# A hybrid decoder step on one core: another way to sum one layer norm's variance, and plain products for one feature pair

## The chip, the cores and the metric

The kernel runs on one core of one Trainium2 chip. The metric is device time in microseconds (us): 1178.86 us, the median of three runs (1178.64 to 1180.99). TensorE is called PE in the profile (PEld is its weight load), VectorE DVE, ScalarE ACT, GpSimd POOL, and SyncE SP, which here issues all DMAs.

## What is computed

One layer of a decoder on 1024 prompt positions and 32 sample positions (8 sequences of 4), model width 1024. Cut to what matters here:

```python
mixed = concat([rms_norm(y_lru, g_lru), rms_norm(y_attn, g_attn)])   # width 1024
y_mix = mixed @ w_out + b_out
h1 = layer_norm(ALPHA * x + y_mix, ln1_g, ln1_b)                     # "first norm"
hid = silu(h1 @ w_gate) * (h1 @ w_up)                                # 2816 features
h2 = layer_norm(ALPHA * h1 + hid @ w_down, ln2_g, ln2_b)
```

`layer_norm` subtracts the mean over the 1024 features, divides by the root of the mean square plus 1e-5, scales and shifts.

## The kernel before, in words

Features lie on the 128 partitions and positions along the free dimension, so a 1024-wide row of activations is eight tiles, `y1[m, s]`. There are two chunks of positions: chunk 0 with 512 positions, chunk 1 with 544 (512 prompt, 32 sample), the latter often handled in two halves of 272, named `10` and `1272`.

Nearly every product is done in three matmuls. An operand is split into a rounded high part (a copy into the type fp32r, by ACT or DVE) and the rest as low part (a subtraction, by POOL or DVE), and `three` adds high by high, high by low and low by high. A split therefore costs one copy and one subtraction.

The order of work: input projections, attention and recurrence; the output projection of chunk 0 and then of chunk 1 (`out_stream`, banks `ps_o`); the first norm of each chunk (`layer_norm1`) followed by `right_factors`; gate and up projection by feature pairs (`gate_up`); the down projection with the second norm (`last_sums`, `norm2`). The first norm of chunk 0 falls into the output projection of chunk 1. The first norm of chunk 1 has no such cover but the first feature pair of chunk 0: `EARLY = 2` lets features 0 and 1 of chunk 0 be done alone, then come features 0 and 1 of chunk 1 alone, then all later pairs with both chunks.

A feature pair is a 256 x 1024 block of weights times the 1024-wide activations. `gate_up` does it by a seven-product scheme: both sides are cut in 2 x 2 blocks, and seven products of sums of blocks (`a11`, `s2`, `s1`, `a12`, `s3`, `s4`, `a22` on the left; `b11`, `e`, `t1`, `b21`, `t3`, `b22`, `t4` on the right), each of four steps of 128, are combined by DVE (`take`). `right_factors` makes the right blocks of one chunk: for each `k` of 0 to 3 it takes the tiles `x = y1[k]` and `y = y1[k + 4]`, forms `t1` and `e` (tile `rf..u`) and `t3` and `t4` (`rf..v`) by four additions or subtractions of half a tile, and splits `y`, `u`, `v` and half of `x`.

In the first norm, `mean_square` sums over the partitions by one matmul with a matrix of 1/1024 (`ones`) and leaves the mean in PSUM (`ps_m1`). DVE centres the eight tiles, ACT squares them, POOL or DVE adds the squares up, and `rstd` brings the sum to one value per position (matmuls with one column each, a root and a reciprocal on small tiles, four small diagonals, and a matmul that spreads the result over the partitions in PSUM, `v1_.._b`). DVE then multiplies the eight tiles by it.

Nothing is issued as written. The functions record operations; a planner (`Recorder.order`) then plays the program through with a cost per operation, a due time taken from the order of matmuls, and the number of buffers, and fixes the order on every engine. `nc.tt` may go to POOL or DVE and `nc.copy` to ACT or DVE: the first engine named is home, and the planner leaves it when it would be late there. The costs know nothing of one engine slowing another. Since one line issues everything (L417), all rows of the profile have that line, and one goes by the names of tiles. In the profile the names are shortened (`x7_b` to `x_b`, `x7_t` to `x_t`, `v1` to `v`).

Buffers that play a part: 73 slots of tag `g` for activations; `wh` and `wl`, two each, for split weights; `wr` (4) and `wq` (5) for raw weights; three PSUM banks `mm`, two `s`, two `tp`.

## Time and profile before

| | |
|---|---|
| median of the runs | 1178.86 us |
| profiled execution, its own time | 1177.26 us |
| its span, first to last instruction | 1175.5 us |
| mean granted clock of TensorE | 0.966 |
| busy: PE, PEld | 1096.3 us (93%), 1020.7 us (87%) |
| busy: DVE, ACT, POOL | 695.3 us (59%), 569.6 us (48%), 767.0 us (65%) |

The busy shares are means over stages with different limits. The granted clock is a share of 2.4 GHz; the two levels are 1.0 and 0.5, and a value between them is a mean over a stretch. DVE and POOL durations hold also the time in which an instruction stands on its engine and can't go on.

### The profile page before, as it was taken

How to read it: one execution, taken by the hardware profiler on the slowest of the kernel's cores; microseconds unless marked ns; L12 is line 12 of the kernel's file. 1: busy time of each engine (PE TensorE's matmuls, PEld its weight loads, DVE VectorE, ACT ScalarE, POOL GpSimd, SP SyncE). 2: the span in 40 equal slices, each digit the busy share in tenths (PEclk: the TensorE clock that was granted, in tenths of full speed). 3: DMA queues.
4: the chain of work that ended last, by engine and by line, in shares of the span. 5: the costliest groups of instructions: out<-in, count | busy, mean ns of one | idle time of the engine just before them, and what ended most of it. 6: DMA issues, size and time to landing. Idle time of an engine off the chain costs nothing.

```text
span 1175.5 us, 20650 instructions
## 1 busy us (share of the span) xinstructions
PE 1096.3 (93%) x7546; PEld 1020.7 (87%) x7546; DVE 695.3 (59%) x1332; ACT 569.6 (48%) x1096; POOL 767.0 (65%) x687
## 2 busy tenths in 40 slices
PE   9789998987998966899999999999999999999996
PEld 7578888875777965899999999999999888899996
DVE  6998847899877599833333324333335644376654
ACT  6578836687744346433233223323335433465553
POOL 7844464566756977898878877887889936501100
PEclk9999999999899968899999999999999999999998
DMA  8420012244133413234223323322338636566561
GB/s 290 148 73 20 27 56 76 76 142 126 64 124 110 136 55 113 91 108 160 99 87 118 127 73 110 118 100 83 119 124 302 209 117 212 159 205 207 180 200 48
DMA packets 83813, 146.59 MB, mean 125 GB/s; under 512 B 12112, under 2 KB 16368, under 8 KB 83696
## 3 DMA queue, kind: packets, MB, share of 16 engines
q1 hardware_dynamic: 83712, 145.28, 37.5%
q8 instruction: 59, 0.97, 0.4%
q14 instruction: 42, 0.34, 0.1%
HBM read 121.75 MB, written 21.80 MB: 122 GB/s over the span
## 4 chain that ended last, share of the span: by engine, by line
PE 64%; DVE 7%; issue 1%; ACT 0%; POOL 0%; DVEq 0%; ACTq 0%
PE ps_d L417 22%; PE ps_o L417 5%; PE ps_7g L417 3%; PE ps_1u L417 3%; PE ps_4g L417 3%; PE ps_6u L417 3%; PE ps_5u L417 3%; PE ps_4u L417 3%; PE ps_3u L417 3%; PE ps_3g L417 3%; PE ps_7u L417 3%; PE ps_2u L417 3%; PE ps_1g L417 3%; PE ps_6g L417 3%; PE ps_5g L417 2%; PE ps_2g L417 2%
## 5 line engine op out<-in xcount | busy, mean ns | idle before, releaser
L417 PE MATMUL ps_d<-hid_h,wd 128*128 128x272 f32 (+1 forms) x1056 | 245.2, 325 | 0.0
L417 PEld LDWEIGHTS ps_d<-hid_h,wd 128*128 128x128 f32 x1056 | 176.7, 188 | 16.0 <-issue 0.5
L417 DVE SCALAR_TENSOR_TENSOR wd<-wd_r,wmean,wd 128x512 fp32r<-128x512 f32 x132 | 116.2, 916 | 107.9 <-ACT wd L417 107.6
L417 PE MATMUL ps_d<-hid_l,wd 128*128 128x272 f32 (+1 forms) x528 | 170.3, 325 | 0.0
L417 ACT ACTIVATE wd<-wd_r,wmean 128x512 fp32r<-128x512 f32 x132 | 90.4, 719 | 93.1 <-PE ps_d L417 83.9
L417 PEld LDWEIGHTS ps_d<-hid_l,wd 128*128 128x128 f32 x528 | 99.0, 188 | 8.4 <-issue 0.5
L417 POOL TENSOR_TENSOR var<-var,q_l 128x272 f32<-128x272 f32 (+1 forms) x17 | 19.6, 1151 | 116.9 <-ACT q_l L417 83.2
L417 POOL TENSOR_TENSOR hid_l<-hr,hid_h 128x512 fp32r<-128x512 f32 (+1 forms) x44 | 63.2, 1451 | 11.9 <-ACT hid_h L417 8.8
L417 PE MATMUL ps_o<-mix_h,wo_h 128*128 128x272 f32 (+1 forms) x192 | 66.6, 350 | 1.3 <-DVE y L417 1.3
L417 PE MATMUL ps_o<-mix_l,wo_h 128*128 128x272 f32 (+1 forms) x192 | 63.6, 333 | 0.6 <-POOL mix_l L417 0.6
L417 PE MATMUL ps_o<-mix_h,wo_l 128*128 128x272 f32 (+1 forms) x192 | 63.8, 334 | 0.1
L417 POOL TENSOR_TENSOR up<-sg,up 128x512 f32<-128x512 f32 (+1 forms) x44 | 59.9, 1362 | 0.0
L417 ACT ACTIVATE p<-p,st 128x257 f32<-128x257 f32 (+3 forms) x104 | 49.5, 490 | 14.6 <-DVE st L417 14.1
L417 POOL TENSOR_TENSOR wo_l<-wo_r,wo_h 128x512 fp32r<-128x512 f32 x31 | 41.7, 1360 | 16.1 <-ACT wo_h L417 16.1
L417 PEld LDWEIGHTS ps_o<-mix_h,wo_h 128*128 128x128 f32 x192 | 37.4, 195 | 4.6 <-DVE y L417 1.5
L417 POOL TENSOR_TENSOR sum<-sum,y 128x272 f32<-128x272 f32 (+1 forms) x33 | 35.6, 1091 | 8.2 <-DVE y L417 7.9
L417 PEld LDWEIGHTS ps_o<-mix_l,wo_h 128*128 128x128 f32 x192 | 37.4, 195 | 3.6 <-POOL mix_l L417 0.8
L417 PE MATMUL ps_1g<-x_b,wg_a11p 128*128 128x256 f32 (+1 forms) x264 | 35.9, 290 | 4.9 <-DVE x_b L417 2.4
L417 PE MATMUL ps_2g<-x_b_h,wg_a12p 128*128 128x272 f32 (+1 forms) x176 | 35.0, 290 | 5.2 <-DVE up L417 5.2
L417 ACT CAST hid_h<-hr 128x512 fp32r<-128x512 f32 (+1 forms) x44 | 27.4, 631 | 25.3 <-DMA hr<-hid 24.5
L417 PEld LDWEIGHTS ps_o<-mix_h,wo_l 128*128 128x128 f32 x192 | 36.9, 192 | 3.0 <-DVE wo_l L417 0.3
L417 DVE TENSOR_TENSOR up<-up,ps_6u 128x256 f32<-128x256 f32 (+1 forms) x22 | 9.4, 428 | 50.1 <-PE ps_6u L417 46.2
(514 smaller groups left out, 3777.0 us busy)
## 6 DMA issues: line engine op xcount, KB each, us to landing
wd_r<-in_dram SPq DMA_DIRECT2D x132, 256.0 KB, 3.0
wg_a<-in_dram SPq DMA_DIRECT2D x48, 256.0 KB, 3.0
wu_a<-in_dram SPq DMA_DIRECT2D x48, 256.0 KB, 2.7
wm<-in_dram SPq DMA_DIRECT2D x44, 256.0 KB, 3.3
wo_r<-in_dram SPq DMA_DIRECT2D x32, 256.0 KB, 2.9
hid<-up SPq DMA_DIRECT2D x22, 272.0 KB, 2.1
hr<-hid SPq DMA_DIRECT2D x22, 272.0 KB, 3.1
hid<-up SPq DMA_DIRECT2D x22, 256.0 KB, 2.1
```

What stands on the lines that cost most here:

```text
L417: getattr(getattr(self.nc, op.eng), op.fn)(*[real(a) for a in op.args], **{k: real(v) for k, v in op.kw.items()})
```

## The change

Two things change. In the first norm of chunk 1 (`if s:`) the squares go straight into matmuls with the 1/1024 matrix, eight accumulated in one PSUM bank; a root over the full 128 x 272 tile on ACT, and a reciprocal on DVE, give the factor as a tile in SBUF. Chunk 0 keeps the old way. And the first feature pair of chunk 0 is done by `gate_up0`: for gate and up and each of the two features, eight plain products of 128 x 128 weights with 512 positions, whose right operands are the split rows (`rows`). So `right_factors(0)` splits whole rows of `x`, not half of them; all the other splits stay, since later pairs still use the seven products. The subtractions of the splits in `right_factors` now have DVE as home, for both chunks.

```diff
--- before.py
+++ after.py
@@ -1197,10 +1197,10 @@
 
     MIX_ORDER = (4, 5, 6, 7, 0, 1, 2, 3)
 
-    def split(dst, y, o, n):
+    def split(dst, y, o, n, first="gpsimd"):
         h, l = dst
         nc.copy(h[:, o : o + n], y)
-        nc.tt(l[:, o : o + n], y, h[:, o : o + n].bitcast(F32), op=ALU.subtract)
+        nc.tt(l[:, o : o + n], y, h[:, o : o + n].bitcast(F32), op=ALU.subtract, first=first)
 
     y1 = {}
     sums = {}
@@ -1241,22 +1241,37 @@
 
         nm = f"{s}{o}"
         mu = mean_square(sums[s, o][:, :n], n, f"ps_m1_{nm}")
-        s2 = [temp(f"v{i}_{nm}") for i in range(2)]
-        for m in range(8):
-            y = y1[m, s][:, o : o + n]
-            i = m % 2
-            nc.vector.scalar_tensor_tensor(y, y, bcen[:, m : m + 1], mu[:, :n], op0=ALU.add, op1=ALU.subtract)
-            q = s2[i] if m < 2 else temp(f"q{m}_{nm}")
-            nc.scalar.activation(q[:, :n], y, AF.Square)
-            if m >= 2:
-                nc.tt(s2[i][:, :n], s2[i][:, :n], q[:, :n], op=ALU.add)
-            if m % 3 == 2:
-                yield
-        nc.tt(s2[0][:, :n], s2[0][:, :n], s2[1][:, :n], op=ALU.add, first="vector")
-        s2 = s2[0]
-        yield
-        r = rstd(s2[:, :n], n, f"v1_{nm}", 1.0, 1e-5)
-        yield
+        if s:
+            var = acc(f"ps_v1_{nm}", pss, "s")
+            for m in range(8):
+                y = y1[m, s][:, o : o + n]
+                nc.vector.scalar_tensor_tensor(y, y, bcen[:, m : m + 1], mu[:, :n], op0=ALU.add, op1=ALU.subtract)
+                q = temp(f"q{m}_{nm}")
+                nc.scalar.activation(q[:, :n], y, AF.Square)
+                nc.tensor.matmul(var[:, :n], ones, q[:, :n], start=(m == 0), stop=(m == 7))
+                if m % 3 == 2:
+                    yield
+            yield
+            r = temp(f"r1_{nm}")
+            nc.scalar.activation(r[:, :n], var[:, :n], AF.Sqrt, bias=col("eps", 1))
+            nc.vector.reciprocal(r[:, :n], r[:, :n])
+        else:
+            s2 = [temp(f"v{i}_{nm}") for i in range(2)]
+            for m in range(8):
+                y = y1[m, s][:, o : o + n]
+                i = m % 2
+                nc.vector.scalar_tensor_tensor(y, y, bcen[:, m : m + 1], mu[:, :n], op0=ALU.add, op1=ALU.subtract)
+                q = s2[i] if m < 2 else temp(f"q{m}_{nm}")
+                nc.scalar.activation(q[:, :n], y, AF.Square)
+                if m >= 2:
+                    nc.tt(s2[i][:, :n], s2[i][:, :n], q[:, :n], op=ALU.add)
+                if m % 3 == 2:
+                    yield
+            nc.tt(s2[0][:, :n], s2[0][:, :n], s2[1][:, :n], op=ALU.add, first="vector")
+            s2 = s2[0]
+            yield
+            r = rstd(s2[:, :n], n, f"v1_{nm}", 1.0, 1e-5)
+            yield
         for m in range(8):
             y = y1[m, s][:, o : o + n]
             nc.vector.tensor_tensor(y, y, r[:, :n], op=ALU.mult)
@@ -1275,6 +1290,7 @@
     normed = [0, 0]
     seven = {}
     kept = {}
+    rows = {}
 
     def right_factors(s):
 
@@ -1291,14 +1307,21 @@
             nc.tt(t4, b21, e, op=ALU.subtract)
             for nm, r in ((("b21", "b22"), y), (("t1", "e"), u), (("t3", "t4"), v)):
                 h, l = slot(f"x7_{nm[0]}{k}{s}_h", F32R), slot(f"x7_{nm[0]}{k}{s}_l", F32R)
-                split((h, l), r[:, :n], 0, n)
+                split((h, l), r[:, :n], 0, n, "vector")
+                if nm[0] == "b21":
+                    rows[k + 4] = h, l
                 for i in range(2):
                     c = slice(i * hw, (i + 1) * hw)
                     seven[nm[i], k, s] = (h[:, c], l[:, c])
-            x7 = slot(f"x7_b11{k}{s}", F32R)
-            h, l = seven["b11", k, s] = (x7[:, :hw], x7[:, hw:n])
-            nc.copy(h, b11)
-            nc.tt(l, b11, h.bitcast(F32), op=ALU.subtract)
+            if s:
+                x7 = slot(f"x7_b11{k}{s}", F32R)
+                h, l = seven["b11", k, s] = (x7[:, :hw], x7[:, hw:n])
+                nc.copy(h, b11)
+                nc.tt(l, b11, h.bitcast(F32), op=ALU.subtract, first="vector")
+            else:
+                rows[k] = slot(f"x7_b1{k}_h", F32R), slot(f"x7_b1{k}_l", F32R)
+                split(rows[k], x[:, :n], 0, n, "vector")
+                seven["b11", k, s] = tuple(r[:, :hw] for r in rows[k])
             for m in (k, k + 4):
                 d = kept[m, s] = spill.tile([P, n], F32, tag=f"y{m}{s}", name=f"keep{m}{s}")
                 nc.sync.dma_start(d, y1[m, s][:, :n])
@@ -1407,6 +1430,35 @@
                 nc.tt(u[s][i], g[s][i], u[s][i], op=ALU.mult)
                 d = hid[f + i, s] = spill.tile([P, SC[s][1]], F32, tag=f"h{f + i}{s}", name=f"hid{f + i}{s}")
                 nc.sync.dma_start(d, u[s][i])
+
+    def gate_up0(f):
+
+        n = SC[0][1]
+        yield 0
+        while 7 not in rows or ("b11", 3, 0) not in seven:
+            tick()
+        g = {}
+        for x, w in (("g", w_g), ("u", w_u)):
+            for i in range(2):
+                ps = bank(f"ps_e{x}{f + i}")
+                for j in range(2):
+                    p, t, c = ((pw, "wr", 4), (pg2, "wq", 5))[j]
+                    r = p.tile([P, HW], F32, tag=t, name=f"we{x}{f + i}{j}_r", bufs=c)
+                    nc.sync.dma_start(r, w[f + i][:, j * HW : (j + 1) * HW])
+                    h, l = piece(f"we{x}{f + i}{j}")
+                    nc.copy(h, r)
+                    nc.tt(l, r, h.bitcast(F32), op=ALU.subtract)
+                    for k in range(4):
+                        c = slice(k * P, (k + 1) * P)
+                        yield three(ps, n, h[:, c], l[:, c], *(q[:, :n] for q in rows[4 * j + k]), j + k == 0,
+                                    j + k == 4)
+                if x == "g":
+                    g[i] = slot(f"sg{f + i}0")[:, :n]
+                    nc.scalar.activation(g[i], ps[:, :n], AF.Silu)
+                else:
+                    nc.vector.tensor_tensor(g[i], g[i], ps[:, :n], op=ALU.mult)
+                    d = hid[f + i, 0] = spill.tile([P, n], F32, tag=f"h{f + i}0", name=f"hid{f + i}0")
+                    nc.sync.dma_start(d, g[i])
 
     def row_mean(f):
 
@@ -1582,7 +1634,7 @@
     def means(f):
         return later(lambda: [row_mean(f + i) for i in range(2)])
 
-    streams += [gate_up(f, (0,)) for f in range(0, EARLY, 2)] + [later(settle)]
+    streams += [gate_up0(f) for f in range(0, EARLY, 2)] + [later(settle)]
     for f in range(0, FT, 2):
         streams += [gate_up(f, both if f >= EARLY else (1,)), means(f)]
     streams += [last_sums(*b) for b in LAST]
```

The planner gives another order. On PE, at the end of the output projection (`ps_o711` is its last bank, the first rows here), the products of chunk 0's pair follow: seven-product banks `ps_1g`, `ps_6g` before, plain banks `ps_eg0` now, with the means `ps_m1` and the sums of squares `ps_v1` of chunk 1's two halves. Before:

```order
L417 MATMUL ps_o711_4704<-mix31_l_3738,wo71_h_4585 128x272
L417 MATMUL ps_o711_4704<-mix31_h_3627,wo71_l_4599 128x272
L417 MATMUL ps_1g00_0_4743<-x7_b1100_4320,wg00_a11p_4661 128x256 x3
L417 MATMUL ps_1g00_0_4743<-x7_b1110_4386,wg00_a11p_4661 128x256 x3
L417 MATMUL ps_1g00_0_4743<-x7_b1120_4415,wg00_a11p_4661 128x256 x3
L417 MATMUL ps_1g00_0_4743<-x7_b1130_4430,wg00_a11p_4661 128x256 x3
L417 MATMUL ps_6g00_0_4769<-x7_t100_h_4405,wg00_s2p_4669 128x256
L417 MATMUL ps_6g00_0_4769<-x7_t100_l_4674,wg00_s2p_4669 128x256
L417 MATMUL ps_6g00_0_4769<-x7_t100_h_4405,wg00_s2p_4669 128x256
L417 MATMUL ps_m1_10_4775<-sum_10_4240,oi_206 128x272
L417 MATMUL ps_m1_1272_4780<-sum_1272_4266,oi_206 128x272
```

And now:

```order
L417 MATMUL ps_o711_4718<-mix31_h_3627,wo71_l_4628 128x272
L417 MATMUL ps_eg0_4749<-x7_b10_h_4316,weg00_4680 128x512
L417 MATMUL ps_eg0_4749<-x7_b10_l_4336,weg00_4680 128x512
L417 MATMUL ps_eg0_4749<-x7_b10_h_4316,weg00_4680 128x512
L417 MATMUL ps_m1_10_4760<-sum_10_4236,oi_206 128x272
L417 MATMUL ps_eg0_4749<-x7_b11_h_4339,weg00_4680 128x512
L417 MATMUL ps_eg0_4749<-x7_b11_l_4357,weg00_4680 128x512
L417 MATMUL ps_eg0_4749<-x7_b11_h_4339,weg00_4680 128x512
L417 MATMUL ps_eg0_4749<-x7_b12_h_4367,weg00_4680 128x512
L417 MATMUL ps_eg0_4749<-x7_b12_l_4383,weg00_4680 128x512
L417 MATMUL ps_eg0_4749<-x7_b12_h_4367,weg00_4680 128x512
L417 MATMUL ps_m1_1272_4779<-sum_1272_4262,oi_206 128x272
```

The place of the means is nearly the same; all plain products of the pair (96 with 512 columns) and the 16 of the variance stand before the first product of chunk 1.

On DVE, around the last two evacuations of the output projection (`y1_71<-..ps_o710`, `ps_o711`) and the first centring of chunk 1 (`y1_01<-..ps_m1_10`). Before:

```order
L417 SCALAR_TENSOR_TENSOR y1_71_4062<-y1_71_4062,ps_o710_4658 128x272
L417 TENSOR_TENSOR x7_t310_l_4720<-rf10v_4671,x7_t310_h_4688 128x512
L417 TENSOR_TENSOR sum_10_4240<-sum_10_4240,y1_71_4062 128x272
L417 TENSOR_TENSOR x7_t320_l_4732<-rf20v_4609,x7_t320_h_4716 128x512
L417 SCALAR_TENSOR_TENSOR y1_71_4062<-y1_71_4062,ps_o711_4704 128x272
L417 TENSOR_TENSOR x7_t110_l_4757<-rf10u_4423,x7_t110_h_4531 128x512
L417 TENSOR_TENSOR rf00v_4767<-y1_40_3179,rf00u_4324 128x256
L417 TENSOR_TENSOR x7_b2110_l_4773<-y1_50_3195,x7_b2110_h_4461 128x512
L417 TENSOR_TENSOR x7_t130_l_4784<-rf30u_4508,x7_t130_h_4764 128x512
L417 TENSOR_TENSOR rf30v_4602<-y1_70_3218,rf30u_4508 128x256
L417 TENSOR_TENSOR wg00_s4_4794<-wg00_s2_4637,wg00_a12_4561 128x512
L417 SCALAR_TENSOR_TENSOR y1_01_3295<-y1_01_3295,ng2_314,ps_m1_10_4775 128x272
```

And now:

```order
L417 TENSOR_TENSOR x7_t300_l_4634<-rf00v_4598,x7_t300_h_4624 128x512
L417 SCALAR_TENSOR_TENSOR y1_61_4060<-y1_61_4060,ps_o610_4607 128x272
L417 SCALAR_TENSOR_TENSOR y1_61_4060<-y1_61_4060,ps_o611_4647 128x272
L417 TENSOR_TENSOR x7_t310_l_4705<-rf10v_4618,x7_t310_h_4697 128x512
L417 SCALAR_TENSOR_TENSOR y1_71_4065<-y1_71_4065,ps_o710_4678 128x272
L417 SCALAR_TENSOR_TENSOR y1_71_4065<-y1_71_4065,ps_o711_4718 128x272
L417 SCALAR_TENSOR_TENSOR y1_01_3295<-y1_01_3295,ng2_314,ps_m1_10_4760 128x272
L417 SCALAR_TENSOR_TENSOR y1_11_3329<-y1_11_3329,ng2_314,ps_m1_10_4760 128x272
L417 SCALAR_TENSOR_TENSOR y1_21_3390<-y1_21_3390,ng2_314,ps_m1_10_4760 128x272
L417 SCALAR_TENSOR_TENSOR y1_31_3427<-y1_31_3427,ng2_314,ps_m1_10_4760 128x272
L417 SCALAR_TENSOR_TENSOR y1_41_3684<-y1_41_3684,ng2_314,ps_m1_10_4760 128x272
L417 SCALAR_TENSOR_TENSOR y1_01_3295<-y1_01_3295,ng2_314,ps_m1_1272_4779 128x272
```

The splits of chunk 0's right factors (`x7_..`) and a sum for the weights (`wg00_s4`), which stood between the two, are gone from there; fourteen of chunk 0's splits stand earlier, among the evacuations from `y1_21` on.

On PE, where the last split of chunk 1's right factors (`x7_t331_l`) is used, in product 7 of gate; products 3 and 4 follow. Before:

```order
L417 MATMUL ps_7g01_1_5351<-x7_t331_h_5319,wg01_s3p_5289 128x272
L417 MATMUL ps_7g01_1_5351<-x7_t331_l_5348,wg01_s3p_5289 128x272
L417 MATMUL ps_7g01_1_5351<-x7_t331_h_5319,wg01_s3p_5289 128x272
L417 MATMUL ps_3g01_1_5371<-x7_b2101_h_5232,wg01_s4p_5327 128x272
L417 MATMUL ps_3g01_1_5371<-x7_b2101_l_5271,wg01_s4p_5327 128x272
```

And now:

```order
L417 MATMUL ps_3g01_1_5211<-x7_b2121_h_5139,wg01_s4p_5171 128x272
L417 MATMUL ps_3g01_1_5211<-x7_b2121_l_5165,wg01_s4p_5171 128x272
L417 MATMUL ps_7g01_1_5167<-x7_t331_l_5222,wg01_s3p_5136 128x272
L417 MATMUL ps_7g01_1_5167<-x7_t331_h_5194,wg01_s3p_5136 128x272
L417 MATMUL ps_3g01_1_5211<-x7_b2121_h_5139,wg01_s4p_5171 128x272
L417 MATMUL ps_3g01_1_5211<-x7_b2131_h_5145,wg01_s4p_5171 128x272
L417 MATMUL ps_3g01_1_5211<-x7_b2131_l_5185,wg01_s4p_5171 128x272
L417 MATMUL ps_3g01_1_5211<-x7_b2131_h_5145,wg01_s4p_5171 128x272
L417 MATMUL ps_4g01_1_5248<-x7_t301_h_5153,wg01_a22p_5188 128x272
```

Behind that split there stood 26 matmuls up to the end of product 4 (`ps_4g01`, twelve of 272 columns), and now 18: part of product 3 has moved ahead.

## Rows read from the trace of the kernel before

**Rows 1.** Windows: PE, PEld, DVE, ACT, POOL busy (count), granted clock, DMA share, GB/s.
```profile
372.00:397.00 25.00, 25.00 (x183) 23.97 (x184) 8.11 (x16) 13.90 (x25) 19.93 (x23) 0.93 0.49 167
397.00:411.00 14.00, 13.48 (x109) 13.27 (x108) 13.66 (x14) 3.43 (x7) 13.95 (x12) 1.00 0.39 112
411.00:447.00 36.00, 25.30 (x131) 22.43 (x129) 35.63 (x61) 18.44 (x43) 27.30 (x24) 0.67 0.14 45
447.00:478.00 31.00, 18.40 (x102) 16.44 (x103) 31.00 (x47) 19.28 (x35) 23.01 (x20) 0.78 0.33 115
433.45:436.87 3.42, 3.42 (x20) 3.42 (x19) 3.42 (x5) 1.10 (x3) 2.79 (x3) 0.50 0.24 77
500.00:520.00 20.00, 20.00 (x166) 20.00 (x166) 5.84 (x14) 7.53 (x14) 19.73 (x16) 1.00 0.29 100
```

**Rows 2.** Chain of work that ended last, pieces in order of time.
```profile
474.98 1.80 DVE x_t_l L417
...
480.71 1.66 PE ps_4g L417 x12
...
899.98 2.93 PE ps_4u L417 x24
```

**Rows 3.** Timeline of DVE: start us, duration us, instruction, count.
```profile
412.77 0.42 DVE L417 SCALAR_TENSOR_TENSOR y<-y,ps_o 128x272 f32<-128x272 f32 x1
...
419.45 1.71 DVE L417 SCALAR_TENSOR_TENSOR y<-y,ng,ps_m 128x272 f32<-128x272 f32 x4
...
440.25 2.87 DVE L417 TENSOR_TENSOR y<-y,v_b 128x272 f32<-128x272 f32 x8 [0.37 <-PE v_b L417]
...
452.97 0.42 DVE L417 TENSOR_TENSOR y<-y,v_b 128x272 f32<-128x272 f32 x1
...
477.04 1.47 DVE L417 TENSOR_TENSOR x_t_l<-rf31v,x_t_h 128x544 fp32r<-128x544 f32 x1
```

**Rows 4.** Timeline of POOL, around the end of the output projection.
```profile
397.44 2.81 POOL L417 TENSOR_TENSOR wo_l<-wo_r,wo_h 128x512 fp32r<-128x512 f32 x2
...
413.28 1.14 POOL L417 TENSOR_TENSOR sum<-sum,y 128x272 f32<-128x272 f32 x1 [1.93 <-DVE y L417]
```

**Rows 5.** Groups by form, DVE, 419.4 to 478.5 us: busy us, mean ns.
```profile
L417 DVE SCALAR_TENSOR_TENSOR y<-y,ng,ps_m 128x272 f32<-128x272 f32 x16 | 6.8, 486 | 0.0
...
L417 DVE TENSOR_TENSOR y<-y,v_b 128x272 f32<-128x272 f32 x16 | 5.9, 427 | 0.4 <-PE v_b L417 0.4
...
L417 DVE TENSOR_TENSOR x_b<-y,x_b 128x272 fp32r<-128x272 f32 x3 | 3.0, 999 | 0.0
...
L417 DVE TENSOR_TENSOR wg_s3p<-wg_s,wg_s3p 128x512 fp32r<-128x512 f32 x2 | 2.5, 1228 | 0.0
...
L417 DVE TENSOR_TENSOR x_b_l<-y,x_b_h 128x544 fp32r<-128x544 f32 x3 | 2.1, 712 | 0.0
...
L417 DVE TENSOR_TENSOR x_t_l<-rf11v,x_t_h 128x544 fp32r<-128x544 f32 x1 | 1.8, 1804 | 0.0
...
L417 DVE TENSOR_TENSOR rf11v<-y,rf11u 128x272 f32<-128x272 f32 x1 | 1.6, 1575 | 0.0
...
L417 DVE TENSOR_TENSOR rf21v<-y,y 128x272 f32<-128x272 f32 x1 | 0.4, 429 | 0.0
...
L417 DVE CAST wg_a12p<-wg_a 128x512 fp32r<-128x512 f32 x1 | 0.9, 906 | 0.0
```

**Rows 6.** Timeline of the last norm, 1162 to 1171 us.
```profile
1162.93 2.00 PE L417 MATMUL ps_var<-q_l,oi 128*128 128x272 f32 x8
...
1165.54 1.85 DVE L417 RECIPROCAL r_last<-r_last 128x272 f32<-128x272 f32 x1 [1.98 <-ACT r_last L417]
...
1167.43 3.33 DVE L417 TENSOR_TENSOR y<-y,r_last 128x272 f32<-128x272 f32 x6
```

**Rows 7.** Timeline of PE in the down projection.
```profile
959.67 0.63 PE L417 MATMUL ps_d<-hid_h,wd 128*128 128x512 f32 x2
...
962.46 0.63 PE L417 MATMUL ps_d<-hid_h,wd 128*128 128x512 f32 x2
```

## The prediction

> **What bounds the kernel now.** I read the chain of waits first, then busy time by windows, then the timelines of the engines that the chain names. From 482.4 us on (480.71 and 1.66) the chain is PE alone, up to the pair that ends at 902.9 [rows 2]; there PE is busy throughout, 20.00 of 20 us at full clock [rows 1]. Only what stands ahead can give something back, and whatever lets PE come earlier to the end of product 4 of gate of chunk 1 (482.4) comes out at the end whole, since the matmuls behind that point are the same before and after. Ahead of it the windows show a hole: PE is busy 25.30 of 36 us and then 18.40 of 31, while DVE is busy 35.63 and 31.00 [rows 1]. DVE sets the pace there. Its timeline shows why [rows 3]: the last evacuation of the output projection comes at 412.77, the first centring of chunk 1 at 419.45, the first multiplications by the root's reciprocal at 440.25, the last at 452.97, and the last split of the right factors ends at 478.5 (477.04 and 1.47). PE then has 3.9 us to the end of product 4.
>
> **A price that decides: two inputs from SBUF.** On DVE, 272 columns with one operand out of PSUM take 0.43 us each, and 16 of them 5.9 [rows 5], so 0.37 elapse per instruction (0.06 less than the duration, as they overlap). With both operands in SBUF the same size takes from 0.43 to 1.58, and 512 or 544 columns from 0.71 to 1.80 [rows 5], while POOL is at work. I read the long ones as DVE and POOL holding each other up. The Trainium skill, SBUF — State Buffer, section Who interferes with whom, says that a DVE instruction with two SBUF inputs contends with a GpSimd instruction that reads SBUF. It speaks against a part of this change, since the norm's factor moves from PSUM to SBUF and all 16 multiplications fall under it; by the rule each could cost as much as the other two-input instructions, some 6 us more in all than I take below. The trace agrees as to the kinds (mean 0.43 against 1.00).
>
> **The norm's part.** Gone from DVE between first centring and last split are the sums of squares, the small roots and reciprocals and the diagonals; the two sums on one column and two spreading matmuls go from PE. Added on DVE are two reciprocals of 128x272 at 1.85 [rows 6]. The 16 multiplications stay, at 0.56 each by the last norm, which has the same form (six in 3.33) [rows 6]; bounds 0.37 and 1.0. Added on PE are 16 matmuls with squares, which the trace counts as two each: 32 at 0.25 (eight in 2.00) [rows 6], 8.0 us.
>
> **The pair's part.** PE: the 168 matmuls of the seven products go, at 0.122 (24 in 2.93) [rows 2] 20.5 us; 96 of 512 columns come, at 0.2325 (twelve between the two rows, 2.79) [rows 7], 22.3 us. That is 1.8 us more, but it lies where PE waits. DVE: 16 combinations and its share of left sums and splits go, two multiplications of 512 out of PSUM come, at 0.69 by columns. Raw weights are eight tiles either way, so SP's loads are the same in number; its writes of normed rows only change places with loads that wait for buffers anyway. I take nothing for them, nor for ACT, which is busy half of each stretch [rows 1]; if a load were late, PE would wait for it.
>
> **The moved splits.** Fourteen subtractions of chunk 0 go to DVE among the evacuations, where it is busy 8.11 of 25 us [rows 1], and leave its queue between the last evacuation and the first centring. So centring need not wait until 419.45. It waits for the sum of chunk 1's tiles on POOL, which before ended at 414.4 (413.28 and 1.14) [rows 4]. POOL's list up to there is about as long as before, so I take 414.5 for the first centring; between 412 (list shorter) and 424 (each of fourteen splits holds POOL for its own 0.71).
>
> **The sum, on DVE.** From first centring to last split there were 96 instructions in 59.1 us (419.45 to 478.5); by the order there are now 61. Sixteen centrings 6.8 [rows 5]; two reciprocals 3.7; 16 multiplications 8.9; seven other two-input instructions of 272 at 0.94 (the mean 1.00 less the overlap) 6.6; fifteen of 512 or 544 at 1.17 (1.23 less the overlap, between ends of 0.65 and 1.74) 17.6; two out of PSUM 1.4; three casts at 0.85 2.6 [rows 5]. Together 47.6. A new wait is in it: the first reciprocal waits for a root on ACT, which stands behind a cast of chunk 0's last right factor (`x_t_h` of `rf30v`), which waits for POOL, eight instructions behind the last sum. At 1.40 for seven and 1.14 for one [rows 4] these end at 425.4; the centrings and one split before end at 422.5. DVE idles 3 us; behind it wait all multiplications, and a plain product of PE whose bank the root frees. The last split then ends at 414.5 + 47.6 + 3 = 465.1, and PE has 18 matmuls left, not 26, at 0.122: 2.2 us, so 467.3 in place of 482.4. Gain 15.1 us. The profiled execution (1177.26) would come to 1162.2; against the median of the runs, 1.6 us above it, 1163.8.
>
> PE must fit under this: from 411, when the output projection is done, 22.3 of plain products, 8.0 of variance, 1.0 of means and 84 matmuls of chunk 1's first products at 0.122, 10.2: 41.5 us, to 452.5 at full clock. It has 15 us to spare.
>
> **Bounds.** With every two-input instruction at its short end the list is 31 us, and POOL binds instead: 31 instructions from its last sum to product 4's weights, 17 at 1.40 and 14 at 1.14, 39.8, to 454.2; end 456.4, 1153. With the fifteen large at 1.74, the seven at 1.5 and the multiplications at 1.0 it is 64.5 us: end 484, and nothing is won.
>
> **Rivals.**
> - *Early contention.* The fourteen splits hold POOL, which is busy 13.95 of 14 us between 397 and 411 [rows 1] and makes the low parts of the output weights there (two in 2.81 [rows 4]); PE starves for them and all that follows is late by up to 9.9 us (14 at 0.71): 1173.7. For it: POOL has no slack. Against: POOL also loses work there, and DVE is as often the one held.
> - *The stall moves.* After the hole POOL is busy 19.73 of 20 us [rows 1]. In the hole it idled 16.7 us (8.70 and 7.99) and could run ahead with weights; in a shorter one of 50.6 with 39.8 of work it idles 10.8. If PE gets that difference, 5.9 us, back as waits for weights, the change does only part of what it says: 1169.7. Against it: in 500 to 520 PE did not wait at all.
> - *The lower clock, slower than before.* PE's work in the hole is now longer and its products stand in one queue with the variance matmuls, which wait for ACT. In the old hole PE ran at 0.67 and 0.78 of full clock, at 0.50 even in a slice of 3.42 us in which it was busy throughout [rows 1], 1.2 instead of 2.4 GHz. Held at the lower level, 41.5 becomes 83 us, and product 4 ends at 494, 11.6 late: 1190.5. It decides from a mean clock of 0.58 down (41.5 over the 71.4 from 411 to 482.4). Against: the more PE has to do the less it idles, and where it was busy without a break the clock was 1.00 [rows 1]. The Trainium skill, TensorE: Matmul & The Clock Gate, section What's actually happening, has the gate open after sustained activity; by it a bound PE would speed up, which the trace bears out.
>
> **Numbers.** Forecast 0.60, own range 1157 to 1170. Early contention 0.15, stall moves 0.13, lower clock 0.06, all else that leaves the time about where it is 0.06. The likeliest time is 1163.8; the range for 8 in 10 is 1155 to 1174, which takes in most of the two rivals on the same side. Within 0.2% (2.4 us) is what a measurement can't tell from no change. Faster takes the first three but a little: 0.86; same 0.06; slower 0.08.
>
> **What would show it.** Right: first centring at 414 to 417 with no split between it and the last evacuation; reciprocals of 1.85 near 426; last split at 460 to 468; PE without waits from there, and nothing changed behind 482 but the shift. Wrong: the end of the output projection later than 412 (early contention); granted clock near 0.5 from 425 to 450 with PE busy throughout (clock); PE waiting for POOL's low parts after 468 (the stall moved); multiplications by the norm's factor near 1 us each (the price of SBUF).

## The result and the profile after

The changed kernel takes 1161.32 us (median of four runs, 1158.94 to 1162.57) against 1178.75 for the one before: ratio 0.9847, 95% interval 0.9826 to 0.9869. In the profiled executions the span falls from 1175.5 to 1159.3, 16.2 us; product 4 of gate of chunk 1 ends at 466.14 instead of 482.37, also 16.2. The whole gain is made ahead of that point, in the hole. The windows of the kernel after, in the columns of [rows 1], show it:

```profile
397.00:411.00 14.00, 11.65 (x87) 10.79 (x86) 5.86 (x9) 3.52 (x6) 14.00 (x16) 1.00 0.23 76
411.00:447.00 36.00, 34.76 (x150) 28.08 (x151) 31.45 (x45) 27.02 (x56) 29.16 (x26) 0.95 0.33 112
447.00:466.00 19.00, 12.91 (x66) 11.23 (x66) 19.00 (x24) 6.65 (x13) 12.74 (x11) 0.64 0.42 141
466.00:484.00 18.00, 18.00 (x148) 18.00 (x147) 10.38 (x21) 8.15 (x15) 18.00 (x15) 1.00 0.32 104
```

Where PE was busy 25.30 of 36 us at a clock of 0.67 [rows 1] it is now busy 34.76 at 0.95. What is left of the hole is 447 to 466, in which DVE is busy throughout. From 466 on PE has no gap. The chain of waits of the kernel after (start us, us, what) enters PE at 459.77; in the kernel before it entered PE at 477.26 (a piece between the first two of [rows 2]):

```profile
459.08 0.65 DVE x_b_l L417
...
459.77 0.82 PE ps_2g L417 x2
...
464.54 1.60 PE ps_4g L417 x12
```

One profile each doesn't give the gain to a microsecond. Up to the first matmul of the output projection the traces of all fourteen kernels of this document show the same instructions in the same order on PE, DVE, ACT and POOL and the same loads, and yet the profiled executions reach it between 254.07 and 260.12 us: that difference doesn't come from the order of work. Call this matmul the mark. PE's timelines, of the kernel before, the kernel after, and a run used below (`variance_twice`):

```profile
256.22 0.48 PE L417 MATMUL ps_o<-mix_h,wo_h 128*128 128x512 f32 x1
258.65 0.48 PE L417 MATMUL ps_o<-mix_h,wo_h 128*128 128x512 f32 x1
254.82 0.48 PE L417 MATMUL ps_o<-mix_h,wo_h 128*128 128x512 f32 x1
```

From the mark, product 4 ends after 226.2 us before and after 207.5 now: 18.7 us are gained, of which 2.4 were lost ahead of the mark in this execution. The ratio of the timed runs makes it 18.0.

DVE's timeline after, the lines that answer to [rows 3]:

```profile
408.15 0.77 DVE L417 SCALAR_TENSOR_TENSOR y<-y,ps_o 128x272 f32<-128x272 f32 x2
411.64 2.13 DVE L417 SCALAR_TENSOR_TENSOR y<-y,ng,ps_m 128x272 f32<-128x272 f32 x5 [2.72 <-PE ps_m L417]
...
423.56 0.69 DVE L417 TENSOR_TENSOR x_t_l<-rf30v,x_t_h 128x512 fp32r<-128x512 f32 x1 [2.50 <-ACT x_t_h L417]
424.34 1.85 DVE L417 RECIPROCAL r<-r 128x272 f32<-128x272 f32 x1
426.22 3.15 DVE L417 TENSOR_TENSOR y<-y,r 128x272 f32<-128x272 f32 x7
...
431.40 6.84 DVE L417 TENSOR_TENSOR y<-y,r 128x272 f32<-128x272 f32 x8
...
440.96 1.01 DVE L417 TENSOR_TENSOR y<-y,r 128x272 f32<-128x272 f32 x1
...
461.54 1.80 DVE L417 TENSOR_TENSOR x_t_l<-rf31v,x_t_h 128x544 fp32r<-128x544 f32 x1
```

The sixteen multiplications take 11.0 us together, and not alike: those beside POOL's work are the long ones (more on that below). The same view of ACT explains the 2.50 us in which DVE idles ahead of the reciprocal: the low part there and the root for the reciprocal both stood behind one cast on ACT, which waited for POOL.

```profile
422.91 0.62 ACT L417 CAST x_t_h<-rf30v 128x512 fp32r<-128x512 f32 x1 [2.16 <-POOL rf30v L417]
423.82 0.49 ACT L417 ACTIVATE r<-ps_v,vt 128x272 f32<-128x272 f32 x1 [0.29 <-PE ps_v L417]
```

Two more views are needed below: what PE waited for from 411 to 484 (engine, tile, releaser: us in total, times, longest). In the kernel before:

```profile
PE ps_2g L417 <- DVE up L417: 5.2, 1, 5.2
PE v_t L417 <- DVE v L417: 3.6, 1, 3.6
...
PE v_b L417 <- DVE v_d L417: 2.1, 1, 2.1
PE ps_1g L417 <- DVE up L417: 2.0, 1, 2.0
PE ps_4u L417 <- DVE up L417: 1.5, 1, 1.5
...
PE ps_6g L417 <- DVE up L417: 0.8, 1, 0.8
...
PE ps_7g L417 <- DVE up L417: 0.4, 1, 0.4
```

In the kernel after, all of it:

```profile
PE ps_2g L417 <- DVE x_b_l L417: 5.5, 4, 2.5
PE ps_m L417 <- POOL sum L417: 2.0, 1, 2.0
PE ps_6g L417 <- DVE x_t_l L417: 1.6, 2, 1.1
```

The waits for `up` (DVE combines chunk 0's seven products out of their banks) went with the pair's part, those for `v_t` and `v_b` with the norm's part. The low parts of chunk 1's right factors remain.

### The profile page after: what moved, and what is told of

Read it like the earlier page. It is cut to its first block, busy times and chain, and to the rows that moved or that the text cites. A ratio compares the mean times of both kernels' runs of the same rounds, so it can differ in the third digit from the quotient of the medians.

```text
span 1159.3 us, 20461 instructions
## 1 busy us (share of the span) xinstructions
PE 1096.1 (95%) x7486; PEld 1017.2 (88%) x7486; DVE 677.7 (58%) x1291; ACT 567.5 (49%) x1088; POOL 753.8 (65%) x676
## 4 chain that ended last, share of the span: by engine, by line
PE 59%; DVE 1%; ACT 0%; DVEq 0%; issue 0%; ACTq 0%
PE ps_d L417 22%; PE ps_7g L417 3%; PE ps_3g L417 3%; PE ps_4g L417 3%; PE ps_2u L417 3%; PE ps_6u L417 3%; PE ps_3u L417 3%; PE ps_4u L417 3%; PE ps_1u L417 3%; PE ps_7u L417 3%; PE ps_5u L417 3%; PE ps_2g L417 3%; PE ps_6g L417 3%; PE ps_1g L417 3%; PE ps_5g L417 3%; DVE y L417 0%
## 5 line engine op out<-in xcount | busy, mean ns | idle before, releaser
L417 POOL TENSOR_TENSOR up<-sg,up 128x544 f32<-128x544 f32 (+1 forms) x42 | 57.0, 1357 | 0.0
L417 DVE TENSOR_TENSOR up<-up,ps_6u 128x272 f32<-128x272 f32 (+1 forms) x21 | 9.0, 430 | 49.9 <-PE ps_6u L417 45.4
L417 DVE TENSOR_TENSOR sg<-sg,ps_6g 128x272 f32<-128x272 f32 (+1 forms) x21 | 9.0, 430 | 49.0 <-PE ps_6g L417 49.0
L417 ACT ACTIVATE sg<-sg 128x544 f32<-128x544 f32 (+1 forms) x42 | 26.9, 644 | 19.4 <-DVE sg L417 19.4
```

Of the source, the lines that this page charges most:

```text
L417: getattr(getattr(self.nc, op.eng), op.fn)(*[real(a) for a in op.args], **{k: real(v) for k, v in op.kw.items()})
```

## The experiments

Ratios are to the kernel before, on the same chip, with 95% intervals.

### The three parts, alone and by twos

The change is taken as three parts: N, the norm of chunk 1; P, the plain products of chunk 0's first pair; S, the home of the low parts on DVE. Each is undone by these edits of the changed kernel (cut to the lines that change, the remarks are mine):

```diff
-        if s:                                   # N undone, in layer_norm1
+        if False:
-            if s:                               # P undone, in right_factors and the streams
+            if True:
                 x7 = slot(f"x7_b11{k}{s}", F32R)
-    streams += [gate_up0(f) for f in range(0, EARLY, 2)] + [later(settle)]
+    streams += [gate_up(f, (0,)) for f in range(0, EARLY, 2)] + [later(settle)]
-                split((h, l), r[:, :n], 0, n, "vector")    # S undone, likewise twice below
+                split((h, l), r[:, :n], 0, n)
```

> Before with the norm's part alone (variance of chunk 1 by matmuls; seven products for the first pair of chunk 0 and the splits on POOL as before). By the order, DVE has 87 instructions from first centring to last split, not 96, but 22 of 512 or 544 columns, not 20. Theory 1, the list of DVE at the prediction's prices, with 0.69 us for a multiplication by the factor in SBUF as measured after the change: centrings 6.8, reciprocals 3.7, multiplications 11, fifteen two-input of 272 14.1, fourteen out of PSUM 5.2, nineteen large 22.2, casts 3.5: 66.5 us, against 58.5 by the same prices before (59.1 measured). First centring near 417, last split near 483: 4 to 5 us slower than before, 1183. Theory 2, the pair's part carries all since it gives PE work in the hole: 1178.8, as before. Theory 3, the gain goes by the number of instructions (0.62 us each): 9 fewer, 1173.

> Before with the pair's part alone (first pair of chunk 0 by eight plain products; norm of chunk 1 and home of the splits as before). By the order DVE has 87 instructions from first centring to last split, 24 large; by prices 55.8 us and some 3 of waits for the small roots. Product 4 of gate of chunk 1, which ended at 482.4 before, at 480.6 with the norm's part alone and at 473.0 with pair and splits. Theory 1, the parts support each other: without the moved splits POOL has the low parts of chunk 0 in the hole again, and product 4 ends near 475: 1171. Rival, the pair's part brings all that pair and splits bring (9 us): 1169 or less; second rival, it brings nothing alone, as norm alone: 1178.

> Before with the low parts of the right factors at home on DVE, and nothing else of the change: norm of chunk 1 and seven products for the first pair of chunk 0 as before. By the order DVE has 98 instructions from first centring to last split, 23 large. Taken out of the whole change, the moved splits cost 8 to 10 us in the timed runs and 3.8 us at product 4. Theory 1, no part is worth anything alone, since the list of DVE stays about as long: 98 instructions against 96, by prices 2 to 4 us longer, with the first centring some 5 us earlier: 1176 to 1180. Rival, the parts add up: 8 to 10 us here as well, 1168 to 1170.

> The changed kernel with the old norm for chunk 1 (sums of squares on DVE, factor spread into PSUM); pair's part and moved splits stay. DVE has 82 instructions from first centring to last split, 19 of them large. Theory 1, by prices: centrings 6.8, small ones 1.2, sixteen two-input of 272 15.0, multiplications out of PSUM 5.9, two more out of PSUM 1.4, thirteen large 15.2, casts 4.8: 50.3, as much as the changed kernel's 51.7, and some 3 us of waits for the two roots: last split near 465, 1163. So the norm's part would be worth about nothing. Rival: the norm's part is worth what its removed instructions measured, 8 to 10 us: 1170.

> The changed kernel with seven products for the first pair of chunk 0, as before; norm's part and moved splits stay. DVE has 81 instructions, 22 large. Theory 1, by prices: 61.8 us from a first centring at 411.6: last split at 473.4, and 26 matmuls of PE behind it: 1173. Theory 2 (the plain products carry all): 1178. Theory 3 (by number, 15 fewer at 0.62, and centring 7.8 earlier): 1162.

> The changed kernel with the low parts of the right factors at home on POOL again; norm's and pair's parts stay. DVE has 66 instructions, 20 large. Theory 1, by prices: 53.6 us and some 3 of waits, first centring near 415 as POOL has the fourteen splits of chunk 0 in front of the sums again: last split near 471, 1169 to 1170. Rival, the home of the splits costs nothing, since DVE and POOL hold each other up wherever they stand: 1161.

Measured; all columns behind the ratio are from the one profiled execution: the mark, start of the first centring, end of DVE's last low part for chunk 1, length of the list between them (by the prices of the expectation, where it gave one), end of product 4, and how long after the mark that is:

| parts | ratio | mark | centring | last low part | list (expected) | product 4 | from the mark |
|---|---|---|---|---|---|---|---|
| none (before) | 1 | 256.22 | 419.45 | 478.51 | 59.1 (58.5) | 482.37 | 226.2 |
| N | 1.0017 (0.9995 to 1.0039) | 254.38 | 410.23 | 475.86 | 65.6 (66.5) | 480.58 | 226.2 |
| P | 1.0000 (0.9981 to 1.0020) | 254.07 | 405.34 | 471.11 | 65.8 (58.8) | 478.31 | 224.2 |
| S | 1.0001 (0.9988 to 1.0013) | 260.12 | 419.94 | 482.54 | 62.6 (61 to 63) | 486.90 | 226.8 |
| N, S | 0.9991 (0.9973 to 1.0009) | 257.38 | 412.58 | 474.49 | 61.9 (61.8) | 479.10 | 221.7 |
| P, S | 0.9924 (0.9897 to 0.9952) | 258.97 | 414.05 | 468.95 | 54.9 (53.3) | 472.96 | 214.0 |
| N, P | 0.9918 (0.9888 to 0.9948) | 254.11 | 404.24 | 464.05 | 59.8 (56.6) | 469.93 | 215.8 |
| N, P, S (after) | 0.9847 (0.9826 to 0.9869) | 258.65 | 411.64 | 463.34 | 51.7 (50.6) | 466.14 | 207.5 |

No part does anything alone; P with either of the others gives half of the gain, all three the whole; N with S gives nothing clear of the noise. "The parts add up" and "the gain goes by the number of instructions" have fallen, and "pair carries all" has fallen too. The gains in the last column agree with the ratios within 3.4 us (1% is 11.8 us), those in the column before it within 4.4, since they also hold how late the execution came to the mark. So a step of two or three us is read from the ratios alone. The prices stood up: every list but P's came out within 0.1 to 3.2 us of its sum (the first was fitted: its prices were read from it). My expected starts didn't: 417 for N (410.23), 415 for N with P (404.24), of which 1.8 and 4.5 us are the mark.

Three traces show what stands in the way where a part is missing.

N without P. PE's waits with N alone: the norm's own (`v_t`, `v_b`) are gone, and PE waits longer for `up` instead, 15.9 us in six lines against 9.9 in the five above. The first:

```profile
PE ps_2g L417 <- DVE up L417: 3.8, 1, 3.8
```

P without S. Chunk 0's other right factors are not needed now before its second pair. The planner puts them behind, on POOL, into the same stretch, and an engine works in order: on ACT the cast of chunk 1's `x_b`, for the first product, stood behind a cast for chunk 0 that waited 6.11 us for POOL. ACT's timeline with P alone:

```profile
469.47 0.62 ACT L417 CAST x_t_h<-rf00v 128x512 fp32r<-128x512 f32 x1 [6.11 <-POOL rf00v L417]
470.00 0.41 ACT L417 CAST x_b<-y 128x272 fp32r<-128x272 f32 x1
```

and PE's: one wait of 7.23 us, which is also the surplus of P's list.

```profile
470.46 0.59 PE L417 MATMUL ps_1g<-x_b,wg_a11p 128*128 128x272 f32 x1 [7.23 <-ACT x_b L417]
```

S without P. Low parts leave the place ahead of the first centring (one is still there), but combinations (`rf..v`) move in. The centring starts at 419.94, 159.8 us from the mark against 163.2 before, and what it gains there the longer list takes back. DVE's timeline with S alone:

```profile
412.15 0.44 DVE L417 SCALAR_TENSOR_TENSOR y<-y,ps_o 128x272 f32<-128x272 f32 x1 [2.58 <-PE ps_o L417]
412.51 0.53 DVE L417 TENSOR_TENSOR rf30v<-y,rf30u 128x256 f32<-128x256 f32 x1
415.03 1.23 DVE L417 TENSOR_TENSOR x_t_l<-rf00v,x_t_h 128x512 fp32r<-128x512 f32 x1 [2.00 <-ACT x_t_h L417]
...
418.51 1.51 DVE L417 TENSOR_TENSOR rf30v<-y,y 128x256 f32<-128x256 f32 x1
419.94 0.89 DVE L417 SCALAR_TENSOR_TENSOR y<-y,ng,ps_m 128x272 f32<-128x272 f32 x2
```

With N and P, and the low parts at home on POOL as before, the centring starts earliest of all, at 404.24 and 150.1 us from the mark (153.0 in the changed kernel): DVE has nothing but evacuations ahead of it. DVE in that kernel:

```profile
403.08 0.44 DVE L417 SCALAR_TENSOR_TENSOR y<-y,ps_o 128x272 f32<-128x272 f32 x1 [2.59 <-PE ps_o L417]
404.24 6.62 DVE L417 SCALAR_TENSOR_TENSOR y<-y,ng,ps_m 128x272 f32<-128x272 f32 x16 [0.72 <-PE ps_m L417]
```

So with N and P in, S does not bring the centring forward: it puts it back by 2.9 us, since DVE now has chunk 0's factors ahead of it. For that its list behind is 8.1 us shorter (59.8 to 51.7). Behind the last low part PE then needs 2.8 us to the end of product 4, and without S 5.9, at a granted clock of 0.58. Together that is 8.3 us from the mark, and 8.4 by the ratios; the 3.8 us between the two ends of product 4 hold a mark that lay 4.5 us earlier without S.

### The price of two inputs from SBUF

```diff
-            r = temp(f"r1_{nm}")
+            r = var
```

> The changed kernel with one edit: the norm's factor stays in the PSUM bank of the variance (root and reciprocal in place), so the 16 multiplications of chunk 1 have one input in SBUF and one in PSUM, as before the change. Nothing else is edited; by the order DVE has 62 instructions in its list, 18 large (61 and 20 in the changed kernel). Theory 1, the price of two SBUF inputs is lost time of DVE: multiplications 5.9 in place of 11.0, the rest by its prices 0.3 shorter; product 4 of gate of chunk 1 ends near 461 (466.1), 1156. Rival: the long multiplications only stand where POOL's work is done, and the same time passes to other instructions of DVE or to POOL: 1160 to 1162.

Measured: 0.9857 (0.9830 to 0.9885), 1161.10: no gain on the changed kernel. The mark lay at 258.77, as in the changed kernel (258.65), so times may be compared as they stand. DVE's timeline of this run:

```profile
426.00 2.86 DVE L417 TENSOR_TENSOR y<-y,ps_v 128x272 f32<-128x272 f32 x8
...
431.21 2.86 DVE L417 TENSOR_TENSOR y<-y,ps_v 128x272 f32<-128x272 f32 x8
...
440.16 1.34 DVE L417 TENSOR_TENSOR x_t_l<-rf01u,x_t_h 128x544 fp32r<-128x544 f32 x1 [2.12 <-ACT x_t_h L417]
...
460.22 1.80 DVE L417 TENSOR_TENSOR x_t_l<-rf31v,x_t_h 128x544 fp32r<-128x544 f32 x1
```

The price is real: 0.36 us elapse per multiplication, 5.7 for sixteen against 11.0, and the last one ends at 434.07, not 441.97. It depends on POOL. In the changed kernel nine multiplications that start while POOL idles (427.26 to 432.45) take 0.43 each; the other seven stand beside POOL's work and take 1.01 to 1.53, six of them between 432.6 and 441.5. With the factor in PSUM they stay at 0.43 though POOL is busy throughout, as the kernel with three edits (below) shows from 430.8 to 433.4. Groups by form in these three stretches (busy us, mean ns):

```profile
L417 DVE TENSOR_TENSOR y<-y,r 128x272 f32<-128x272 f32 x9 | 3.3, 431 | 0.0
L417 DVE TENSOR_TENSOR y<-y,r 128x272 f32<-128x272 f32 x6 | 6.8, 1184 | 0.0
L417 DVE TENSOR_TENSOR y<-y,ps_v 128x272 f32<-128x272 f32 x8 | 2.9, 430 | 0.0
```

It is worth nothing at the end: the last low part ends 1.3 us earlier, product 4 at 466.49 (466.14). First, DVE comes earlier to a point where it waits, 2.12 us, for a cast on ACT, and POOL's combinations, which these casts need, end no earlier: after the change the last `u` is made by 442.6, here by 443.1. Second, the planner fills DVE again. It makes five of the `rf..v` there, three after the change, and behind the last low part the low part of a weight for product 4 itself (`wg_a22p`, until 463.69), which after the change POOL had made by 457.90. So this run bears the rival out, and does not show what the multiplications would be worth if DVE's list were left as it is. POOL's timeline in this run,

```profile
433.33 0.78 POOL L417 TENSOR_TENSOR rf01u<-y 128x272 f32<-128x272 f32 x1 [2.34 <-ACT y L417]
```

and in the changed kernel:

```profile
433.66 0.97 POOL L417 TENSOR_TENSOR rf01u<-y 128x272 f32<-128x272 f32 x1
...
441.63 0.98 POOL L417 TENSOR_TENSOR rf31u<-rf31u,y 128x272 f32<-128x272 f32 x1
```

POOL's own instruction takes 0.97 beside multiplications from SBUF and 0.78 beside those out of PSUM. The Trainium skill, SBUF — State Buffer, section Who interferes with whom, says that a DVE instruction with two SBUF inputs contends with a GpSimd instruction that reads SBUF, and one with at most one SBUF input, outside the two-port modes, does not; the trace agrees, on both engines.

### PE's room in the hole

```diff
-                nc.tensor.matmul(var[:, :n], ones, q[:, :n], start=(m == 0), stop=(m == 7))
+                nc.tensor.matmul(var[:, :n], ones, q[:, :n], start=(m == 0), stop=False)
+                nc.tensor.matmul(var[:, :n], ones, q[:, :n], start=False, stop=(m == 7))
```

> The changed kernel with every variance matmul of chunk 1 issued twice into the same bank (and the root's scale halved): 16 matmuls more, 32 as the trace counts them, 8 us more of PE in the hole; DVE's list by the order has 61 instructions, as without. Theory 1, PE has slack there (6.1 us of waits in 447 to 466 alone, 1.2 in 430 to 447, at a clock of 0.64): 0 to 2 us later, since only the last variance matmuls stand ahead of the roots: 1161 to 1163. Rival, PE's work sets the end of the hole too: all 8 us, 1169.

Measured: 0.9914 (0.9880 to 0.9947), 1167.96, as the rival had it: 6.6 of the 8 us. The four runs spread from 1161.45 to 1170.65, and the profiled one is the fastest; in it product 4 ends at 467.87, only 1.7 later. But that execution came to the mark 3.8 us earlier than the changed kernel's (254.82), and to the first centring 5.3 earlier, though the two kernels issue the same in the same order up to there. From first centring to the end of product 4 it took 61.5 us, the changed kernel 54.5: 7.0 of the 8 us are there too. Of these, 5.1 come ahead of the first reciprocal, which waits 7.38 us for the root, since PE is full ahead of it.

```profile
406.38 6.71 DVE L417 SCALAR_TENSOR_TENSOR y<-y,ng,ps_m 128x272 f32<-128x272 f32 x16 [2.69 <-PE ps_m L417]
...
424.18 1.85 DVE L417 RECIPROCAL r<-r 128x272 f32<-128x272 f32 x1 [7.38 <-ACT r L417]
```

So PE had next to no room for this work, and not the 15 us that I had reckoned: a matmul ahead of the root is on the path, whatever the total of PE's work leaves free behind it.

### Looking for more

```diff
             t1, e, t3, t4 = u[:, :hw], u[:, hw:n], v[:, :hw], v[:, hw:n]
+            home = "gpsimd" if s else "vector"
-            nc.tt(t1, b11, b12, op=ALU.subtract)              # and the three below it
+            nc.tt(t1, b11, b12, op=ALU.subtract, first=home)
```

> The changed kernel with the sixteen additions and subtractions for the right factors of chunk 0 at home on DVE, not POOL. POOL was busy throughout from 385 to 411 with them, the low parts of the output weights and the sums; DVE idled there some 2.7 and 3.3 us at a time behind the casts that wait for them. List by the order 58 instructions, 16 large, some 2 us shorter by prices. Theory 1, POOL's queue ahead of the first centring sets when the hole's list starts: output projection ends near 404, first centring near 406, product 4 ends near 460, 1155. Rival: DVE has 7 to 12 us more ahead of the first centring and holds up its evacuations instead: first centring at 411 to 414, 1160 to 1164.

Measured: 0.9891 (0.9870 to 0.9912), 1164.64, slightly slower than the rival's 1160 to 1164. The first centring came at 413.79, not 406 (mark at 258.50): DVE, with the combinations, was late with its evacuations (the last starts at 412.63, at 408.50 in the changed kernel).

The next adds the factor in PSUM, and for chunk 1 the old home of the low parts (one of the two lines):

```diff
-                split((h, l), r[:, :n], 0, n, "vector")
+                split((h, l), r[:, :n], 0, n, "gpsimd" if s else "vector")
```

> The changed kernel with three edits: factor in PSUM, combinations of chunk 0 at home on DVE, and the low parts of chunk 1's right factors at home on POOL again (those of chunk 0 stay on DVE). DVE's list is then 55 instructions, 14 large: by prices 38 us and some 4 of waits, against 49.7 and 3.8. Theory 1, DVE's list and its start set the end: last split near 450, but POOL then binds, with some 40 us from the last sum to product 4's weights: product 4 near 456, 1150. Rival: what is taken from DVE comes back on POOL at 1.2 us a split, 1158 to 1161.

Measured: 0.9843 (0.9824 to 0.9861), 1158.12; product 4 at 462.23, span 1155.3. The profile is 4.0 us shorter than the changed kernel's (3.2 at product 4 from the mark); the ratios can't tell the two apart. It lies with the rival: DVE's list falls to 45.1 us, and its start moves to 413.48. PE's waits are now

```profile
PE ps_6g L417 <- DVE x_t_l L417: 3.8, 1, 3.8
PE ps_2g L417 <- DVE x_b_l L417: 1.3, 1, 1.3
PE ps_7g L417 <- DVE x_t_l L417: 1.2, 1, 1.2
```

Two more on top of it (in the first, the `yield` behind every second multiplication now counts by `i`):

```diff
-        for m in range(8):                            # multiplications_by_pairs
+        for i, m in enumerate((0, 4, 1, 5, 2, 6, 3, 7) if s else range(8)):
-EARLY = 2                                             # second_plain_pair
+EARLY = 4
```

> The kernel with three edits, and the multiplications of chunk 1 by the factor in the order 0, 4, 1, 5, 2, 6, 3, 7, as the combinations need them in pairs. DVE idled 3.9 us from 433.5 on in the run with three edits, behind ACT's scaling and POOL's combinations (first at 433.2), which need the tiles 0 and 4 of both halves. Theory 1, the chain from multiplication over ACT and POOL to the low parts sets the hole's end now: combinations start 1 to 2 us earlier, 1156 to 1157. Rival, DVE and POOL are full behind it anyway: 1158.

Measured: 0.9832 (0.9796 to 0.9869), 1159.12; product 4 at 463.02. No difference from the kernel with three edits.

> The kernel with three edits (factor in PSUM, combinations of chunk 0 on DVE, chunk 1's low parts on POOL) and the second pair of chunk 0 by plain products as well. PE has 22.3 us more in the hole, 20.5 less behind it. In the run with three edits PE was through its plain products at 442.4, and product 4 ended at 462.2 where 84 matmuls alone would end at 452.6: some 10 us of waits and lower clock to fill. Theory 1, PE is what could still be filled: product 4 ends near 475, the rest follows 20.5 earlier, gain up to 8: 1150. Rival, POOL and DVE set the pace: eight more low parts (1.28 us each on POOL, 10.2) stand in the hole, and behind it a second lone pair of chunk 1 needs 14 low parts and 8 sums in 10.5 us of PE for gate and as much for up: 1160 to 1168.

Measured: 0.9839 (0.9795 to 0.9882), 1159.79; no difference either. This kernel computes a wrong first output (why was not found out), so it is no candidate, and its time is read only as that of this order of work. Product 4 ends at 485.51, 23.3 us later (21.2 from the mark), and from there to the down projection 20.0 are saved. Its windows:

```profile
411.00:447.00 36.00, 36.00 (x168) 29.88 (x167) 18.70 (x39) 27.04 (x55) 21.01 (x19) 1.00 0.45 150
447.00:466.00 19.00, 19.00 (x84) 15.43 (x84) 10.06 (x12) 7.53 (x13) 18.60 (x18) 1.00 0.38 126
466.00:484.00 18.00, 14.25 (x81) 12.70 (x80) 18.00 (x20) 5.48 (x11) 15.62 (x11) 0.83 0.49 162
```

PE is full to 466, at full clock, and it waits for DVE and POOL behind that all the same, 3.8 us: the combinations for chunk 1 (first at 449.43 on POOL) had slid behind the low parts of plain weights.

## Why the prediction came out right, step by step

The forecast was 1163.8 (gain 15.1 at product 4), measured 1161.3 (16.2, and 18.7 from the mark).

- **DVE bounds the hole**: borne out for the kernel before. PE's waits from 411 to 484 came to 23.2 us, 20.1 of them for DVE; after they are 9.1, 7.1 of them for DVE.
- **The three terms**, from the mark: the first centring comes 10.2 us earlier (forecast 5.0), the list is 7.4 shorter (8.5), and PE's work behind the last low part 1.1 (1.7). The list and PE's end were sized well; the start was worth twice what I gave it, and the gain with it some 3 us more.
- **The sum on DVE**: 47.6 and 3 of waits, measured 51.7 from first centring to last low part. The same prices, with the multiplications at the 0.69 measured here, hit the lists of the other kernels but P's. Low by 2.1 were the multiplications (8.9, measured 11.0). By the rule of the Trainium skill, SBUF — State Buffer, section Who interferes with whom, some 15 was my estimate; the trace lies between, since nine of the sixteen met an idle POOL. How much the difference was worth, the run with the factor in PSUM leaves open.
- **The wait for the root**: 3 us expected behind the cast of `rf30v`; 2.50 found at just that cast, first reciprocal at 424.34 (425.4).
- **The moved splits**: the step failed. The centring did wait for the sum on POOL, as forecast (411.64, forecast 414.5), but not because fourteen splits left DVE's queue. From the mark that brings 3.4 us alone, and costs 2.9 with N and P in; N alone brings 7.4, P alone 12.0. That 411.64 lies near 414.5 is luck: P clears the same place, and without S the start would be earlier still. What S is worth lies behind the centring, in the shorter list.
- **PE under it**: 22.3 + 8.0 + 1.0 from 411 gave 442.3, and PE came to chunk 1's first product at 442.4. The step to 15 us of room failed: 8 us more ahead of the root cost 7.0.
- **The rivals**: early contention was small. S makes the output projection end 0.9 us later from the mark than N with P alone (last evacuations end at 408.92 and 403.52, the marks are at 258.65 and 254.11); the rival had up to 9.9. The stall did not move in the changed kernel (PE 18.00 of 18 and 20.00 of 20 behind 466). The clock was 0.95 and 0.64, not 0.5 throughout. It is not free: from 459.77 on the chain is PE alone, 37 matmuls in 6.37 us, and at the 0.122 of full clock it would be 4.5 by my estimate.
- **The bounds**: the upper sum, 64.5, leaves out the three casts (2.6); with them it is 67.1, and the change would have lost some 4 us there. The lower one comes to 33, not 31, and POOL binds there either way.
- **What I had not seen**: I costed the parts one by one, and each is worth nothing by itself. The sum held because all three were in.

## What to carry to other kernels

When one engine feeds a hole through several waits in a row, taking away one wait only lengthens the next; cost the hole's whole list on that engine, not the edit. Time taken off an engine is worth nothing where a planner fills it again, so read the new list before paying for the edit. Room in an engine's total is no room ahead of the instruction that others wait for. Work that a change makes less urgent does not vanish: look where the planner puts it, and what stands behind it in order. And before reading a few microseconds off two profiles, find the last instruction up to which both kernels issue the same, and count from there.

## What the runs showed of the hardware

Of sixteen multiplications of 128x272 with both inputs in SBUF nine, which started while POOL idled, took 0.43 us each, and seven beside a busy POOL 1.01 to 1.53; with one input in PSUM they took 0.43 beside a busy POOL too. POOL's own 272-column instruction went from 0.78 to 0.97 beside DVE's work from SBUF. The granted clock was 1.00 over 55 us in which PE was busy throughout (411 to 466 with the second plain pair), and 0.64 where it waited a third of the time (447 to 466 after). And fourteen executions that issue the same came to the same matmul, some 256 us in, up to 6 us apart.
